# A hybrid decoder trunk on one core: triangles for the solve leave in two parts and are fetched by ScalarE

## The chip, the core and the metric

The kernel runs on one core of a Trainium2 chip. The core has five engines that run side by side, each with a queue of its own that is worked off in order: TensorE (PE, with its weight loads as PEld), VectorE (DVE), ScalarE (ACT), GpSimd (POOL) and SyncE (SP). SP does nothing but issue DMAs here; ACT and POOL can issue DMAs too, from their own queues. A DMA waits in the queue of the engine that issues it, and what stands behind it in that queue waits as well. The metric is device time in microseconds; less is better.

## The reference

One inference step of a two-layer trunk. Layer 0 is sliding-window attention, layer 1 is RWKV-7 time mixing, each between an RMS norm and a residual add, with a last RMS norm behind both. A prompt of 2048 tokens with 16 learned meta tokens ahead of it, and eight decoding sequences of four tokens, both go through it. The change lies in the recurrence of layer 1, which is by token and head

```
S_t = S_{t-1} diag(w_t) + (S_{t-1} a_t) b_t^T + v_t k_t^T ;   y_t = S_t r_t
```

with 16 heads of 64 by 64 states. Behind it y is normalised by head (mean and variance over 64 values, "group norm"), scaled, shifted, a bonus times v is added, the sum is multiplied by a SiLU gate and projected out, and the final norm follows.

## The kernel before

The kernel has four stages: attention, the mixing of neighbouring tokens, the dense projections of the recurrence's inputs, and the recurrence with all that stands behind it. The change is in the last one and in the helpers that it shares with the third.

**Units and chunks.** The recurrence is worked in units of 128 tokens: unit 0 holds the meta tokens, units 1 to 16 the prompt (`us`), and the decoding sequences follow at the end. A unit has four chunks of 32 tokens (unit 0 has one). Within a chunk the recurrence is a triangular system: `scores` (L948) multiplies keys and queries of two chunks at a time (`c2` is 0 or 1), copies the strictly triangular part of the result for each head to the tile `LAs` on ACT (L969) and, after a `yield`, writes the masked rest back into `L` on DVE.

**The inversion.** `inverse` (L976) inverts the 64 triangles of a unit (16 heads by 4 chunks, 32 by 32 each) at once. To have one triangle per partition it writes `LAs` to DRAM (`la_d`, L982 to L984, two DMAs from ACT), reads it back as `LA` into two halves of the partitions (L1007; on SP from unit 3 on), reads the norms `ln` and an identity `X` (L1008, L1010), multiplies `LA` by `ln` (L1009), and does the substitution row by row with two small operations each (`XT`, `X`, L1025 and L1026), on POOL for the units in question. At the end it scales `X` and writes it to DRAM (`tt_d`, L1030). `load_TT` (L1335) reads it back as `TT`, which the solve of the unit needs. `inverse` is a generator: it yields before the read back and at rows 8, 16, 22 and 26, and what stands between two yields is one portion.

**The serial part.** `chain` (L1425) is one chunk: products with the state into `C`, a copy `R0s` on ACT, then `solve` (L1397), small products with `TT` and four copies into `Z` on ACT, then the new state from `LS` and `Z`. `LS` are the keys, transposed on PE by `keys` (L1377) and copied by ACT, eight copies for two chunks; they are ahead of the solves that need them.

**What lies around it.** `steady` (L1770) writes out the order of units 2 to 14. For unit i and its chunk ch it interleaves: the chain of i; the scores of unit i+2, `s` in the code (c2 = 0 at the end of the second chunk, c2 = 1 in the third); the inversion of unit i+1, started while unit i-1 was worked, in its last portions, and of unit i+2 in its first ones; the group norm of unit i-1 (`group_norm`, L1587, in portions that end with MARK); the gate of unit i-1 (`gate`, chunks 2 and 3) and the projection out of unit i-2 (`project_out`, chunks 0 and 1), which are most of PE's work. Two tiles `vt` (L1595) hold v for the group norm; the next unit's loads wait until the last sums (L1643) have read them.

**What sets the order.** The kernel is written in one order, and a planner with a model of the engines' times then places the instructions of each engine. From unit 2 on `in_order` (L1757) ties DVE, ACT and POOL to the order as written, ACT's DMA issues among them; PE and SP are left to the planner. `released()` (L1408) holds what is written under it back, in the plan, until the last instructions of the chain have been issued. So the order on SP is the planner's and is fixed when the kernel is built; on the chip an instruction of SP that waits holds all behind it.

Of the kernel before, what the change touches and what calls it, by code (L numbers as in the profile page):

```python
# [30 lines left out]
def tile_hybrid_step(ctx: ExitStack, tc: tile.TileContext, a, o, c):  # L31
# [916 lines left out]
    def scores(u, c2):  # L948
# [22 lines left out]
        for e in range(2):  # L971
            for cc in range(w):
                r0 = 64 * cc
                tt(v_, L[OS[e], e, cc], pss[e][r0:r0 + 64], mk[r0:r0 + 64, None, :].broadcast_to([64, KC, 64]), ALU.mult)

    def inverse(u, room=None, ln=None):  # L976

        nch = u.nch
        nl = nch * 16
        la_d = dramr.tile([2, nl // 2, 32, 32], F32, name="la_d", tag=f"la_d{nch}")  # L980
        u.tt_d = tt_d = dramr.tile([32, 4, 4 * nch * 32], F32, name="tt_d", tag=f"tt_d{nch}")
        for e in range(2):  # L982
            dma(la_d[e].rearrange("l j i -> j l i"),
                u.LAs[32 * e:32 * e + 32].rearrange("p h c g i -> p (h c g) i"), s_)  # L984
        yield
        eng = v_ if u.idx == 1 else g_
        if u.kind == "m":
            room = wl.tile([P, 2, 32 * 32], F32, name="roomm", tag="L", bufs=nbuf["L"])
        if room is not None:
            LA = room[:, 0].rearrange("p (j i) -> p j i", i=32)  # L990
            XX = room[:, 1].rearrange("p (a k i) -> p a k i", a=2, i=32)
        else:

            LA = wk.tile([P, 32, 32], F32, name="LA", tag="LA", bufs=2)
            XX = None
        if XX is None:
            X = wk.tile([P, 16, 32], F32, name="X", tag="X", bufs=2)
            XT = wk.tile([P, 16, 32], F32, name="XT", tag="XT")
        else:
            X, XT = XX[:, 0], XX[:, 1]  # L1000
        if ln is None:
            ln = wp.tile([P, 32], F32, name="ln", tag=("mu", "rst0")[u.idx % 2])
        if nch < 4:
            g_.memset(LA, 0.0)
            g_.memset(ln, 1.0)
        for hh in range(2):
            dma(LA[hh * 64:hh * 64 + nl], la_d.rearrange("e l j i -> (e l) j i"), s_ if u.idx < PRE else None)  # L1007
            dma(ln[hh * 64:hh * 64 + nl], ln_d[u.idx].rearrange("q c g i -> (q c g) i"))  # L1008
        tt(eng, LA, LA, ln.unsqueeze(2).broadcast_to([P, 32, 32]), ALU.mult)  # L1009
        dma(X, c["laneid"])  # L1010

        low = 16 if u.kind == "m" else 0

        part = {2: 16}.get(u.idx, 0)
        cut = [(v_, 0, part), (g_, part, 16)] if 0 < part < 16 else [(v_, 0, 16)] if part else [(eng, 0, 16)]
        for j in range(low, 31):
            if j in (8, 16, 22, 26):
                yield
            w = 3 - j % 4 if u.kind == "s" else 31 - j
            for eng, k0, k1 in cut if w else ():  # L1020
                ks = slice(max(low // 2, k0), min(j // 2 + 1, k1))
                shape = [P, ks.stop - ks.start, w]
                if shape[1] <= 0:
                    continue
                tt(eng, XT[:, ks, :w], LA[:, j:j + 1, j + 1:j + 1 + w].broadcast_to(shape), X[:, ks, j:j + 1].broadcast_to(shape), ALU.mult)  # L1025
                tt(eng, X[:, ks, j + 1:j + 1 + w], X[:, ks, j + 1:j + 1 + w], XT[:, ks, :w], ALU.add)  # L1026
        for eng, k0, k1 in reversed(cut):
            u.inverted = tt(eng, X[:, k0:k1], X[:, k0:k1], ln[:, None, :].broadcast_to([P, k1 - k0, 32]), ALU.mult)
        for hh in range(2):
            dma(tt_d[hh:32:2].rearrange("k q (l i) -> (q l) k i", i=32), X[hh * 64:hh * 64 + nl])  # L1030
# [11 lines left out]
    with ExitStack() as ph:  # L1042
# [144 lines left out]
        for x, b in enumerate(order):  # L1187
# [39 lines left out]
            if follow is None:  # L1227

                if delay:
                    todo.append((b, prv))  # L1230
                    rest_v = rest_values()
                    fill(rest_v, V0)
                wrx.close()
                es = wrx.enter_context(tc.tile_pool(name="es", bufs=1, side="right", reuse_waits="tile"))
                wl = wrx.enter_context(tc.tile_pool(name="wl", bufs=1, side="right", reuse_waits="tile"))
                for u in us[:PRE]:
                    for _ in load_vectors(u):
                        pass
                if nblk > 2:
                    banks = lambda u: [pd.tile([P, KC, 64], F32, name="pz", tag="pd") for _ in range(2)]  # L1240
                    las = wk.tile([P, 2048], F32, name="las", tag="dx", bufs=1)
                    room1 = wk.tile([P, 2, 1024], F32, name="room1", tag="xn", bufs=1)
                    for i, x0, room in ((1, 0, room1), (0, 1024, None)):
                        u = us[i]
                        u.LAs = las[:64, x0:x0 + 256 * u.nch].rearrange("p (h c g i) -> p h c g i", h=2, g=4, i=32)
                        for c2 in range(u.np):
                            all_of(scores(u, c2))
                        for _ in inverse(u, room, las[:, x0 + 1024 - 32:x0 + 1024] if i == 0 else las[:, 1536:1568]):
                            pass
            if follow is not None:  # L1250
# [18 lines left out]
    with ExitStack() as ph:  # L1269
# [71 lines left out]
        def elementwise(u):  # L1341
            load = idle() if u.L else load_vectors(u)
            next(load, None)
            small_loads(u)
            if u.tt_d is None:
                new_LAs(u)
                for c2 in range(u.np):
                    all_of(scores(u, c2))
                    next(load, None)
                    yield 0.8  # L1350
                for _ in inverse(u):
                    pass
            load_TT(u)
            yield 0.8
# [22 lines left out]
        def keys(u, c2):  # L1377

            w = min(2, u.nch - 2 * c2)
            if u.kind == "s":  # L1380
                u.LS[c2] = [u.room[:, 1]]
            else:
                u.LS[c2] = [LSs[(LScount[0] + cc) % 4] for cc in range(w)]
                LScount[0] += 2
            pss = [pz.tile([P, 4, 2, 64], F32, name="kt", tag="pz") for _ in range(2)]
            for half, ps in enumerate(pss):
                for j in range(4):
                    t_.transpose(out=ps[:w * 64, j].rearrange("p e d -> p (e d)"),
                                 in_=u.BK[half][:, j, 2 * c2:2 * c2 + w, :].rearrange("p c x -> p (c x)"), identity=ident)
            yield  # L1390
            for half, ps in enumerate(pss):
                hs = slice(half * 4, half * 4 + 4)
                for cc in range(w):
                    for e in range(2):
                        act(u.LS[c2][cc][OS[e], e, hs, :], ps[cc * 64:cc * 64 + 64, :, e, :])

        def solve(u, ch, Z, R0s, out):  # L1397

# [371 lines left out]
        def steady(i, u, pe):  # L1770
# [9 lines left out]
            for ch in range(4):  # L1780
# [4 lines left out]

                left = rests[::-1]
                del rests[:]
                if ch == 3:
                    run(norm)
                with released():  # L1790
                    if ch == 2:
                        next(inv.get(i + 1, idle()), None)
# [19 lines left out]
                        run(gen)  # L1812
                if ch == 2:
                    with released():
                        inv[s.idx] = inverse(s)
                        next(inv[s.idx])
                        all_of(sc)
                run(pe[ch], 1.2)
                next(rec)
                with released():  # L1820
                    if ch == 0:
                        kt = keys(u, 1) if i > 2 else idle()
                        next(kt, None)
                        first = L0s.pop(s.idx, None)
                        load_BK(s)
                        s.L.append(first or load_L(s, 0))
                        all_of(kt)
                    if ch == 3:
                        all_of(kt)
                        next(inv[s.idx])  # L1830
                    else:
                        next(inv.get(i + 1, idle()), None)
                if ch < 2:
                    run(norm, to=MARK)
                elif ch == 3:
                    run(norms_[u.idx], to=MARK)
                run(pe[ch], 1.9)
                next(rec, None)
                with released():
# [3 lines left out]
                    if ch == 2 and i + 1 in inv:  # L1843
                        load_TT(us[i + 1])
                if ch == 2:
                    norms_[u.idx] = group_norm(u)
                    run(norms_[u.idx], to=MARK)
                    if ch == 3 and i + 3 < len(us):
                        L0s[i + 3] = load_L(us[i + 3], 0, s_)
# [3 lines left out]
                if ch == 1:  # L1853
                    with released():
                        new_LAs(s)
                        all_of(scores(s, 0))
                rests.append(pe[ch])
                for part in PLAN.get((i, ch), ()):
                    with released():
# [214 lines left out]
```

## Time and profile before

| | |
|---|---|
| Time, median of 3 runs | 2522.64 us (2521.0 to 2528.43) |
| The profiled execution's own time | 2526.93 us |
| Its span in the profile | 2525.2 us |
| Busy share of PE, DVE, ACT, POOL | 89%, 66%, 46%, 41% |
| Mean granted clock of PE | 0.958 |
| Instructions | 60868 |

In the profile's rows a tile name stands with an arrow to what it was made from, so `LA<-la_d` is the fetch of the triangles and `LA<-LA,ln` the first operation of an inversion; `xN` counts instructions. A row of the timeline gives start and duration in microseconds, engine, line, operation and shape, and in square brackets how long the engine had stood idle ahead of it and what it was put down to. ACTq and SPq are the queues of ACT and SP that issue DMAs; their durations are those of the issue, not of the transfer. A row of windows gives, for one stretch, its length, the busy time and number of instructions of PE, PEld, DVE, ACT and POOL, then PE's granted clock, the DMA engines' mean busy share and GB/s. A row of waits gives total, number of times and the longest one. Many lines are helpers: L38 is any matmul, L41 any activation, L44 any tensor_tensor, L47 any scalar_tensor_tensor, L50 any DMA. A wait for several things is put down to the one that came last by the profile, which can be the wrong one. The profile is of one execution and its times don't add up to those of another.

### The profile page before, as it was taken

To read this page: it belongs to the slowest core of one execution; us is meant where nothing else is said; L and a number is where in the kernel's file an instruction comes from. 1 tells how busy PE (TensorE), PEld (TensorE's weight loads), DVE (VectorE), ACT (ScalarE), POOL (GpSimd) and SP (SyncE) were. 2 spreads that over 40 slices of the span, in tenths; PEclk is the share of its full clock that TensorE was granted. 3 is DMA by queue.
4 is the path that set the end of the run, shared out by engine and by line. 5 is a ranking of instruction groups with operands and counts; after the bars stand their busy time and mean duration, and the time that the engine had idled before them with its cause. 6 is when DMAs were issued, how large, how long until landed. Compare 5 with 4: busy or idle time off the path is not lost. (4 is left out here: it accounts for less than half of the span.)

```text
span 2525.2 us, 60868 instructions
## 1 busy us (share of the span) xinstructions
PE 2238.5 (89%) x24932; PEld 1539.7 (61%) x24932; DVE 1666.3 (66%) x3181; ACT 1169.9 (46%) x2799; POOL 1035.9 (41%) x1572
## 2 busy tenths in 40 slices
PE   6989989899989897899999999666898888888897
PEld 5877768677855445577776668444555555555553
DVE  6586674577656987866556656555666666666674
ACT  6675465566432433554343444333444444445431
POOL 4242132333111334543333334314776766767613
PEclk9999999999999998899999999777999999999998
DMA  9433122333247564432222222575555655655323
GB/s 207 126 105 108 64 80 80 112 99 100 98 130 224 198 223 164 138 85 89 96 85 93 98 81 92 162 199 156 130 122 143 147 122 143 144 130 155 94 61 75
DMA packets 346234, 312.98 MB, mean 124 GB/s; under 512 B 205546, under 2 KB 282218, under 8 KB 344131
## 3 DMA queue, kind: packets, MB, share of 16 engines
q1 hardware_dynamic: 302515, 286.15, 38.4%
q10 hardware_dynamic: 41824, 19.15, 3.6%
q0 software_dynamic: 1616, 3.79, 0.7%
q8 instruction: 196, 3.21, 0.5%
q14 instruction: 83, 0.68, 0.1%
HBM read 191.15 MB, written 119.84 MB: 123 GB/s over the span
## 5 line engine op out<-in xcount | busy, mean ns | idle before, releaser
L38 PEld LDWEIGHTS <-yp 128*128 128x128 f16 x1488 | 141.4, 99 | 166.5 <-issue 13.4
L47 DVE SCALAR_TENSOR_TENSOR xm<-dx,mu,xn 128x256 f32<-128x256 f32 (+2 forms) x432 | 199.6, 521 | 48.4 <-POOL dx L44 47.1
L44 POOL TENSOR_TENSOR X<-X,XT 128x126 f32<-128x126 f32 (+24 forms) x458 | 186.1, 406 | 35.7
L44 POOL TENSOR_TENSOR XT<-LA,X 128x126 f32<-128x126 f32 (+24 forms) x458 | 179.7, 392 | 40.4 <-issue 6.7
L38 PE MATMUL pd<-xp,wq 128*128 128x256 f16 (+2 forms) x1728 | 186.7, 267 | 10.4 <-DVE qp L47 8.0
L38 PE MATMUL pd<-wg,xg 128*128 128x512 f16 (+1 forms) x816 | 193.5, 385 | 0.0
L38 PE MATMUL po<-wo,yp 128*128 128x512 f16 x768 | 191.3, 392 | 0.0
L38 PE MATMUL pd<-wvv,xpr 128*128 128x512 f16 (+1 forms) x816 | 189.1, 389 | 0.0
L38 PE MATMUL pd<-xpr,w 128*128 128x256 f16 (+2 forms) x1728 | 186.3, 267 | 0.0
L38 PE MATMUL pd<-xp,wg 128*128 128x256 f16 (+2 forms) x1728 | 181.9, 266 | 1.3 <-DVE xp L44 0.9
L38 PEld LDWEIGHTS <-wq 128*128 128x128 f16 x1728 | 159.5, 99 | 32.9 <-DVE qp L47 9.5
L38 PE MATMUL pd<-xpr,wkk 128*128 128x256 f16 (+2 forms) x1728 | 179.5, 264 | 0.0
L44 POOL TENSOR_TENSOR ssb<-ssb,bias 128x512 f32<-128x512 f32 x64 | 86.3, 1354 | 225.9 <-DVE ssb L462 185.4
L38 PEld LDWEIGHTS <-w 128*128 128x128 f16 x1728 | 157.8, 99 | 27.1 <-issue 9.7
L38 PEld LDWEIGHTS <-wg 128*128 128x128 f16 x1728 | 158.8, 99 | 21.7 <-issue 4.5
L38 PEld LDWEIGHTS <-wkk 128*128 128x128 f16 x1728 | 158.2, 98 | 15.6 <-issue 0.4
L38 PE MATMUL pd<-w,yp 128*128 128x512 f16 x720 | 162.3, 383 | 4.4 <-DMA yp<-y 4.4
L44 POOL TENSOR_TENSOR ps<-wst,ps 128x1024 f16<-128x1024 f32 x32 | 69.4, 2169 | 219.6 <-ACT wst L41 195.7
L44 DVE TENSOR_TENSOR Z<-C,pe 64x256 f32<-64x256 f32 x256 | 108.0, 422 | 61.0 <-PE C L38 42.9
L38 PEld LDWEIGHTS <-xpr 128*128 128x128 f16 (+1 forms) x816 | 79.2, 100 | 103.0 <-issue 18.3
L44 DVE TENSOR_TENSOR xpr<-xm,xpr 128x512 f16<-128x512 f32 (+2 forms) x144 | 98.9, 708 | 56.9 <-ACT xpr L41 56.6
L41 ACT ACTIVATE ssb<-ssb,ng 128x128 f32<-128x128 f32 (+1 forms) x272 | 104.2, 384 | 58.5 <-DVE es L44 54.8
(357 smaller groups left out, 4686.0 us busy)
## 6 DMA issues: line engine op xcount, KB each, us to landing
wst<-in_rwkv_w_in SPq DMA_DIRECT2D x32, 512.0 KB
wsp<-ps SPq DMA_DIRECT2D x32, 512.0 KB
BK<-bk SPq DMA_DIRECT2D x32, 512.0 KB
x<-in_x_prompt SPq DMA_DIRECT2D x29, 512.0 KB
xn<-xn SPq DMA_DIRECT2D x14, 1028.0 KB
ar<-aro SPq DMA_DIRECT2D x28, 512.0 KB
bk<-bko SPq DMA_DIRECT2D x28, 512.0 KB
L<-ar SPq DMA_DIRECT2D x38, 256.0 KB
```

The lines of the kernel that those rows point to most:

```text
L38: return t_.matmul(out=out, lhsT=lhsT, rhs=rhs, start=start, stop=stop, **kw).ins
L41: return s_.activation(out=out, in_=in_, func=func, **kw).ins
L44: return e.tensor_tensor(out=out, in0=in0, in1=in1, op=op).ins
L47: v_.scalar_tensor_tensor(out=out, in0=in0, scalar=scalar, in1=in1, op0=op0, op1=op1)
```

## The change

Four things in one edit.

- A new helper, `lanes_out`, writes the triangles to DRAM in two parts, one for each pair of chunks, each part as four DMAs (two row groups by two halves of the heads) where there were two for the whole unit. In `steady` the first part leaves at the end of the second chunk, ahead of the masked write-back, and the second part in the third chunk. For prompt units above 3 (`inner`: index over PRE, which is 3) they are issued by SP, for the others by ACT as before.
- `inverse` loads `ln` and the identity first and then yields; the read of `LA` comes in a second portion, which for `inner` units is issued by ACT, in the third chunk of unit i behind its solve, and then yields again. The multiplication of `LA` and the first rows stay in the fourth chunk.
- The last portion of the group norm, the sums with `vt`, moves from the start of the fourth chunk to the end of the third, ahead of the loads of the next `vt`.
- `keys` yields after each half of its copies. In a unit's first chunk the second half now comes after the portion of the group norm that has the squares and the variance.

```diff
+    def lanes_out(u, parts):
+
+        nl = u.nch * 16
+        if 0 in parts:
+            u.la_d = dramr.tile([2, nl // 2, 32, 32], F32, name="la_d", tag=f"la_d{u.nch}")
+        for c2 in parts:
+            w = min(2, u.nch - 2 * c2)
+            for e in range(2):
+                for h in range(2):
+                    l0 = (h * u.nch + 2 * c2) * 4
+
+                    dma(u.la_d[e, l0:l0 + 4 * w].rearrange("l j i -> j l i"),
+                        u.LAs[32 * e:32 * e + 32, h, 2 * c2:2 * c2 + w].rearrange("p c g i -> p (c g) i"), None if inner(u) else s_)
+
+    def inner(u):
+        return PRE < u.idx and u.kind == "p"
+
     def inverse(u, room=None, ln=None):
...
-        la_d = dramr.tile([2, nl // 2, 32, 32], F32, name="la_d", tag=f"la_d{nch}")
+        la_d = u.la_d
...
-        for e in range(2):
-            dma(la_d[e].rearrange("l j i -> j l i"),
-                u.LAs[32 * e:32 * e + 32].rearrange("p h c g i -> p (h c g) i"), s_)
-        yield
...
         for hh in range(2):
-            dma(LA[hh * 64:hh * 64 + nl], la_d.rearrange("e l j i -> (e l) j i"), s_ if u.idx < PRE else None)
             dma(ln[hh * 64:hh * 64 + nl], ln_d[u.idx].rearrange("q c g i -> (q c g) i"))
+        dma(X, c["laneid"])
+        yield
+        for hh in range(2):
+            dma(LA[hh * 64:hh * 64 + nl], la_d.rearrange("e l j i -> (e l) j i"), s_ if inner(u) or u.idx < PRE else None)
+        if inner(u):
+            yield
         tt(eng, LA, LA, ln.unsqueeze(2).broadcast_to([P, 32, 32]), ALU.mult)
-        dma(X, c["laneid"])
...
                     for e in range(2):
                         act(u.LS[c2][cc][OS[e], e, hs, :], ps[cc * 64:cc * 64 + 64, :, e, :])
+                yield
...
                 del rests[:]
-                if ch == 3:
-                    run(norm)
...
                 if ch == 2:
                     with released():
+                        lanes_out(s, (1,))
                         inv[s.idx] = inverse(s)
                         next(inv[s.idx])
                         all_of(sc)
...
-                        all_of(kt)
+                        next(kt, None)
                     if ch == 3:
                         all_of(kt)
                         next(inv[s.idx])
                     else:
                         next(inv.get(i + 1, idle()), None)
+                    if ch == 2 and s.idx > PRE:
+                        next(inv[s.idx])
                 if ch < 2:
                     run(norm, to=MARK)
+                if ch == 0:
+                    with released():
+                        all_of(kt)
                 elif ch == 3:
                     run(norms_[u.idx], to=MARK)
...
                 if ch == 2:
+                    run(norm)
                     norms_[u.idx] = group_norm(u)
...
                 if ch == 1:
                     with released():
                         new_LAs(s)
-                        all_of(scores(s, 0))
+                        sc = scores(s, 0)
+                        next(sc)
+                        lanes_out(s, (0,))
+                        all_of(sc)
```

Where `inverse` is called for units 0 to 3 outside `steady` (L1248 and L1351), a call of `lanes_out` for the parts now stands ahead of it, in `elementwise` after each pair of scores.

More of the change, by code (lines that the diff above doesn't have):

```diff
@@ L1247, in tile_hybrid_step @@
                             all_of(scores(u, c2))
+                        lanes_out(u, range(u.np))
                         for _ in inverse(u, room, las[:, x0 + 1024 - 32:x0 + 1024] if i == 0 else las[:, 1536:1568]):
@@ L1348, in elementwise @@
                     all_of(scores(u, c2))
+                    lanes_out(u, (c2,))
                     next(load, None)
```

## The prediction

> **What bounds the kernel now.** I read the page first, for which stage is long and what its chain is made of.
>
> ```profile
> span 2525.2 us, 60868 instructions
> PE 2238.5 (89%) x24932; PEld 1539.7 (61%) x24932; DVE 1666.3 (66%) x3181; ACT 1169.9 (46%) x2799; POOL 1035.9 (41%) x1572
> POOL 4242132333111334543333334314776766767613
> POOL 12%; PE 7%; DMA 5%; issue 3%; SPq 2%; DVE 1%; ACT 1%; ACTq 0%; POOLq 0%; DVEq 0%
> ```
>
> PE is busiest over the whole span, but the chain that ended last is mostly POOL. POOL is near 70% busy in slices 28 to 37 alone: that is the recurrence. Next come the groups on tile LA from 1750 us on, the busy times of the eleven units that lie between its first and its twelfth multiplication, and the waits of PE in the same stage.
>
> ```profile
> L44 POOL TENSOR_TENSOR LA<-LA,ln x13: 1910/1912/1914, 1761.7 to 2320.1; 128x1024 f32<-128x1024 f32 x13
> ...
> 1761.70:2274.20 512.50, 450.62 (x8374) 272.61 (x8369) 343.01 (x552) 233.66 (x592) 359.82 (x759) 0.97 0.56 135
> ```
>
> ```profile
> PE C L38 <- DMA TT<-tt_d: 21.8, 13, 3.3
> PE yps L1676 <- DVE gt L44: 13.8, 12, 1.2
> PE C L38 <- issue: 12.6, 9, 1.9
> PE C L38 <- ACT Z L41: 10.1, 14, 1.3
> ```
>
> Thirteen inversions start from 1761.7 to 2320.1, so a unit takes 558.4/12 = **46.53 us**. In the eleven whole units PE is busy 450.62/11 = 41.0 us each, POOL 32.7. The four waits, from 1750 to 2280 us (530/46.53 = 11.4 units), are 1.9, 1.2, 1.1 and 0.9 us of PE per unit: with the 41.0 they make 46.1, nearly the whole unit. Now one unit in order of time on POOL, SP, ACT, PE and DVE.
>
> ```profile
> 1985.47 1.28 POOL L44 TENSOR_TENSOR X<-X,ln 128x512 f32<-128x512 f32 x1
> 1994.84 1.91 POOL L44 TENSOR_TENSOR LA<-LA,ln 128x1024 f32<-128x1024 f32 x1 [8.08 <-DMA Z<-v]
> ...
> 2011.61 0.20 POOL L1623 TENSOR_SCALAR var<-var 128x16 f32<-128x16 f32 x1 [0.40 <-DVE var L1620]
> ...
> 2031.81 1.27 POOL L44 TENSOR_TENSOR X<-X,ln 128x512 f32<-128x512 f32 x1
> ```
>
> ```profile
> 1986.78 1.36 SPq L50 DMA_DIRECT2D tt_d<-X  x2
> 1988.19 1.33 SPq L50 DMA_DIRECT2D ln<-ln  x2
> 1989.63 1.17 SPq L50 DMA_DIRECT2D LA<-la_d  x2
> 1990.90 1.10 SPq L50 DMA_DIRECT2D TT<-tt_d  x2
> ...
> 1992.57 1.06 SPq L50 DMA_DIRECT2D vt<-v  x2
> ```
>
> ```profile
> 1980.21 0.94 ACTq L50 DMA_DIRECT2D la_d<-LAs  x2
> 1981.19 1.56 ACT L41 ACTIVATE Z<-C 32x256 f32<-32x256 f32 x4 [1.01 <-issue]
> 1985.58 0.60 ACT L41 ACTIVATE gt<-pd 128x512 f32<-128x512 f32 x1 [2.82 <-PE pd L38]
> ...
> 2006.61 2.32 ACT L41 ACTIVATE LS<-kt 64x256 f32<-64x256 f32 x6 [0.21 <-PE kt L1388]
> ...
> 2009.62 0.58 ACT L41 ACTIVATE Y<-ytm 128x512 f32<-128x512 f32 x1
> ```
>
> POOL ends one inversion at 1986.75 and then stands 8.08 us until the next unit's triangle is in LA. The wait is put down to Z<-v, but LA's own DMA explains it: the triangle left for DRAM at 1980.21 from the ACT queue, and its fetch was issued on SP only at 1989.63, because SP's queue stood behind tt_d<-X, which needs the end of the inversion before. The single microseconds below show that the triangle had been moved by then: the DMA engines are busy from 1981 to 1983 and empty after it.
>
> ```profile
> 1982.00:1983.00 1.00, 0.87 (x20) 0.73 (x22) 0.49 (x2) 0.74 (x2) 0.84 (x3) 1.00 0.56 91
> 1983.00:1984.00 1.00, 1.00 (x19) 0.66 (x17) 0.97 (x3) 0.00 (x0) 0.77 (x4) 1.00 0.00 0
> ...
> 1992.00:1993.00 1.00, 1.00 (x14) 0.46 (x14) 0.97 (x3) 0.96 (x3) 0.00 (x0) 1.00 1.11 279
> ```
>
> A second loop has almost the same length; these are its rows on PE and DVE.
>
> ```profile
> 1988.88 0.66 PE L1676 MATMUL yps<-ident,gt 128*128 128x128 f32 x4 [1.15 <-DVE gt L44]
> ...
> 2002.08 1.06 PE L38 MATMUL C<-R0s,TT 32*32 32x64 f32 x28 [3.33 <-DMA TT<-tt_d]
> ```
>
> ```profile
> 1986.21 0.69 DVE L47 SCALAR_TENSOR_TENSOR gt<-gt,pd 128x512 f32<-128x512 f32 x1 [1.74 <-ACT gt L41]
> 1986.81 1.28 DVE L44 TENSOR_TENSOR ytm<-ytm,vt 128x512 f32<-128x512 f32 x2
> 1988.13 0.69 DVE L44 TENSOR_TENSOR gt<-gt,ytm 128x512 f32<-128x512 f32 x1
> ...
> 2006.38 1.41 DVE L44 TENSOR_TENSOR ytm<-Y,mean 64x512 f32<-64x512 f32 x2
> 2010.23 1.29 DVE L1620 TENSOR_REDUCE var<-Y 128x8 f32<-128x512 f32 x2 [2.44 <-ACT Y L41]
> ```
>
> From the inversion's end at 1986.75 its result goes out as tt_d and back as TT, and PE can solve at 2002.08: 15.3 us. From there to the end of the variance's reduction on DVE at 2011.52 it is 9.4. POOL, whose next operation in its order is that variance, then needs until 2033.08, 21.5. Together 46.2: POOL waited only 0.40 us at var, so this **TT loop** ties with the LA wait. Removing the LA wait alone would only move POOL's stand to var.
>
> **The change, part by part.** *The fetch.* For units 4 to 16 LA<-la_d leaves SP, and is issued on ACT between the third chunk's Z copies (end 1982.75) and its gate (1985.58). The second part's four writes, now on SP, wait for copies that end at 1980.2. Their price: a pair of the same bytes took 0.94 us to issue, so 0.9 to 1.9 for four, I take 1.3 (about 0.3 each); and by the rows above some 2 us to land: 1983.5. The fetch is 1.17 to issue and was in use 5.2 us after its issue (1989.63 to 1994.84): 1988.7, which is 2.0 after the inversion's end, not 8.1. The first part's writes leave a chunk earlier and are covered by the scores and solve of that chunk. ACT is held for the landing from 1982.75 to about 1983.5 and needs 1.2 for the issue, inside its 2.82 wait for PE; queued behind it are gt, R0s and everything of the fourth chunk, so this cover is thin. SP's eight small writes cost it 2.6 us of issue per unit while nothing else is due.
>
> *Around TT.* With LA's two reads (512 KB) off SP's queue, TT no longer lies behind them: at 279 GB/s (row 1992) that is up to 1.9 us. ln and laneid also go before tt_d now; the 1.33 and 1.17 us of issue between tt_d and TT may have been covered by tt_d's own landing, so they are worth 0 to 2.5. Against it, vt is free earlier, and its 512 KB could go out ahead of tt_d: a loss of up to 1.9. Ends -1.9 and +4.4, I take a gain of 1.0: that of half of LA's bytes.
>
> *Squares.* Eight key copies take 3.1 us (2.32 for six); the squares now follow the first four, so the first starts at about 2006.61 + 1.55 = 2008.16, when ytm is ready (2007.79), not at 2009.62: 1.5 us earlier, with the var behind it. The four later copies then end 1.2 us later, which their reader, the state update, can bear or not: 0 to 1.2, I take 0, since in this unit that update was waiting for po's matmuls around it.
>
> *The last sums.* The two additions of vt (1.28) go from between the gate's two DVE steps to the idle 1.74 ahead of them. The product is ready 1.3 earlier and PE's wait of 1.15 at yps goes: 1.2 per unit on PE, 0 if another wait takes its place.
>
> *Start.* Units 0 to 3 keep ACT for everything, and their triangles now go in four DMAs per part. For units 0 and 1 that is 8 more on the path to the first solve.
>
> ```profile
> 1604.74 1.01 ACTq L50 DMA_DIRECT2D la_d<-las  x2
> 1606.20 4.39 ACTq L50 DMA_DIRECT2D la_d<-las  x2
> 1610.93 1.14 ACTq L50 DMA_DIRECT2D room<-la_d  x2
> ```
>
> At 0.3 to 0.5 each this is 2.4 to 4.0; part of it may vanish in the 4.39, where ACT's queue waited anyway. Ends 0 and 4, I take a loss of 2.0.
>
> *The sum.* Three limits for the new unit. PE: 41.0 busy, none of which the change removes; with the waits for TT and yps gone but the other two and small ones kept (about 2.2): 43.2. TT loop: 14.3 + 7.9 + 21.5 = 43.7. LA, over two units: from TT's arrival to the second part's writes 26.7 (2002.08 to the next unit's 2028.8, below), 8.5 for out and back as above, 38.2 of POOL (1994.84 to 2033.08), 14.3 for TT's trip: 87.7, or 43.9 for one.
>
> ```profile
> 2028.79 0.94 ACTq L50 DMA_DIRECT2D la_d<-LAs  x2
> ```
>
> I take the longest, 43.9: a gain of 2.6 in each of 12 units, 31.6, less 2.0 at the start, **29.6 us**. The profiled execution took 2526.93 (span 2525.2, 1.7 around it) and would take 2497.3; the median of the runs shown lies 4.3 lower, so 2493.
>
> By the Trainium skill (DMA: Bandwidth & Descriptors, "Issuing engines are not separate DMA queues") DMAs from SP and ACT run on the same 16 engines, and issuing from two of them saves just the time of issue. That speaks against expecting more than 1.17 us a unit here; but the rows show a wait in SP's order, not a shortage of engines (none busy in 1983). Its result is the fourth rival.
>
> **The rivals.** *Better.* TT's trip shrinks by more than 2 and PE's remaining waits halve as units close up: PE is at 41.0 + 1.1 = 42.1, a gain of 4.4 x 12 - 2 = 51: 2472. For it: PE's other waits are called issue and Z, which are matters of order. Against: PE would be 97% busy, as it is nowhere in this stage.
>
> *Hidden anyway.* POOL reaches var early and stands there, because TT's trip stays at 15.3 and the squares wait for something else. For it: the loop's 46.2 against 46.5 today. Then only a few tenths, say 0.5 a unit, are left: 2522.6 - 6 + 2 = 2519.
>
> *Slower.* The change doesn't do what it says: the planner puts the second part's writes behind tt_d in SP's order. Then SP holds them until 1986.75, they are out at 1989.4 and landed at 1991.4, LA is there at 1996.6 instead of 1994.8, and ACT, which stands at the fetch, lets the gate through at 1992.6 and not 1985.6. POOL's part alone is 1.8 x 12 + 2: 2546, more if PE starves. It loses from the point where the writes land later than 1989.6, today's issue of the fetch. For it: SP stands in order for long.
>
> ```profile
> SPq L50 <- POOL X L44: 94.0, 11, 10.3
> ...
> SPq L50 <- DMA la_d<-LAs: 9.4, 1, 9.4
> ```
>
> Against: in the code these writes come before the third chunk's solve, and POOL's last steps are released only after it, so tt_d should be planned later.
>
> *Issue time only.* If the transfers stay as slow as now and only SP's 1.17 of issue is saved per unit: 14 - 2 = 12, 2511.
>
> **How the numbers follow.** Forecast 0.58, better 0.10, hidden 0.15, slower 0.11, issue only 0.06. The forecast's own range is a unit of 43.2 to 45.0: 2485 to 2506. About 0.3% (7.6 us) is what a measurement of this kernel can tell from no change. Faster by more: the forecast, better, issue only, and half of hidden, 0.81. Within: the other half, 0.08. Slower: 0.11. The range 2474 to 2522 takes in half of better and all of hidden and leaves out slower: about 0.16 outside.
>
> **What would show it.** LA multiplications 43 to 45 us apart; POOL's idle time before LA 2 us or less, with some of it now before var; LA<-la_d on the ACT queue before tt_d<-X on SP; PE's wait at yps near zero, at TT smaller; the squares among the LS copies. The forecast is wrong if the unit stays above 45.5 although POOL no longer waits at LA (then the TT loop did not shrink), if ACT's wait before gt grows past 3 us with the fetch in front of it, or if the gain is lost between 1600 and 1700 us.

## The result and the profile after

The changed kernel takes 2508.43 us in the median of four runs, the kernel before 2523.29 in the same comparison: a ratio of 0.993, 95% interval 0.9916 to 0.9944, so about 15 us less. The forecast was 2493, some 30 less. The profiled execution took 2505.96 us, 21.0 less than that of before; it lies 2.5 under its median, that of before 3.6 over its own, so the two profiles differ by more than the medians do.

The page of the changed kernel:

```profile
span 2504.2 us, 61036 instructions
PE 2247.1 (90%) x24932; PEld 1543.8 (62%) x24932; DVE 1676.0 (67%) x3181; ACT 1169.6 (47%) x2799; POOL 1035.7 (41%) x1572
POOL 4242132233111333533333333314677777777613
```

PE's and POOL's work are the same; the slices of the recurrence are fuller. The inversions of units 4 to 16, and POOL's waits from 1768 to 2246 us, of the changed kernel (the columns of a wait are total, times, longest):

```profile
L44 POOL TENSOR_TENSOR LA<-LA,ln x13: 1910/1912/2104, 1765.9 to 2300.3; 128x1024 f32<-128x1024 f32 x13
```

```profile
POOL LA L44 <- DMA LA<-la_d: 36.4, 8, 5.9
POOL var L1643 <- DVE var L1640: 14.2, 9, 2.2
POOL LA L44 <- DMA TT<-tt_d: 6.7, 1, 6.7
POOL LA L44 <- DMA ln<-ln: 5.0, 1, 5.0
```

and those of the kernel before in the same stretch:

```profile
POOL LA L44 <- DMA Z<-v: 68.7, 8, 9.1
POOL LA L44 <- DMA LA<-la_d: 16.6, 2, 8.8
POOL var L1623 <- DVE var L1620: 1.5, 2, 1.1
```

A unit takes 534.4/12 = 44.53 us where it took 46.53. POOL's wait at LA fell from 85.3/10 = 8.5 to 48.1/10 = 4.8 us a unit, and a new stand at var came in, 1.4 where there was 0.2. One unit of the changed kernel on POOL, SP, ACT, PE and DVE:

```profile
2158.46 1.26 POOL L44 TENSOR_TENSOR X<-X,ln 128x512 f32<-128x512 f32 x1
2163.98 1.91 POOL L44 TENSOR_TENSOR LA<-LA,ln 128x1024 f32<-128x1024 f32 x1 [4.26 <-DMA LA<-la_d]
...
2182.23 0.20 POOL L1643 TENSOR_SCALAR var<-var 128x16 f32<-128x16 f32 x1 [1.92 <-DVE var L1640]
...
2202.75 1.27 POOL L44 TENSOR_TENSOR X<-X,ln 128x512 f32<-128x512 f32 x1
2208.47 1.91 POOL L44 TENSOR_TENSOR LA<-LA,ln 128x1024 f32<-128x1024 f32 x1 [4.44 <-DMA LA<-la_d]
```

```profile
2159.75 1.57 SPq L50 DMA_DIRECT2D tt_d<-X  x2
2161.38 2.65 SPq L50 DMA_DIRECT2D ln<-ln  x2
2166.15 1.09 SPq L50 DMA_DIRECT2D TT<-tt_d  x2
...
2194.12 2.95 SPq L50 DMA_DIRECT2D la_d<-LAs  x4
...
2199.00 3.00 SPq L50 DMA_DIRECT2D la_d<-LAs  x4
```

```profile
2178.78 1.55 ACT L41 ACTIVATE LS<-kt 64x256 f32<-64x256 f32 x4
2180.23 0.58 ACT L41 ACTIVATE Y<-ytm 128x512 f32<-128x512 f32 x1
...
2199.78 1.56 ACT L41 ACTIVATE Z<-C 32x256 f32<-32x256 f32 x4
2203.52 1.11 ACTq L50 DMA_DIRECT2D LA<-la_d  x2
2204.68 0.60 ACT L41 ACTIVATE gt<-pd 128x512 f32<-128x512 f32 x1 [3.34 <-PE pd L38]
```

```profile
2174.05 0.64 PE L38 MATMUL C<-R0s,TT 32*32 32x64 f32 x28 [2.07 <-DMA TT<-tt_d]
```

```profile
2180.85 1.29 DVE L1640 TENSOR_REDUCE var<-Y 128x8 f32<-128x512 f32 x2 [0.61 <-ACT Y L41]
```

The fetch of the triangles stands on ACT at 2203.52, ahead of the inversion's end at 2204.02 and not behind it, as meant. The TT loop can be read off: from the inversion's end (2159.72) to PE's solve 14.3 us, to the end of the variance on DVE (2182.14) 8.1, to the next inversion's end 21.9, together 44.3, which is the unit. POOL stood 1.92 us at var in it, so in this unit the TT loop ended last, and the wait at LA did not.

Three lengths serve for all runs below. They count from the last product of the projections, `k<-aa,k` on POOL, since the stages ahead of it are the same code in all kernels and yet end up to 15 us apart (1583.5 to 1598.5).

```profile
1589.56 0.73 POOL L44 TENSOR_TENSOR k<-aa,k 128x256 f32<-128x256 f32 x1 [2.71 <-ACT aa L41]
```

```profile
1587.02 0.73 POOL L44 TENSOR_TENSOR k<-aa,k 128x256 f32<-128x256 f32 x1 [2.71 <-ACT aa L41]
```

(Kernel before, then changed kernel.) "Start" runs from there to LA of unit 4, "unit" is a twelfth of the time from there to LA of unit 16, "end" runs from there to the end of the span. All ratios are against the kernel before on the same chip.

| kernel | start | unit | end | ratio | 95% interval |
|---|---|---|---|---|---|
| before | 172.2 | 46.53 | 205.1 | 1 | |
| changed | 178.9 | 44.53 | 203.9 | 0.9930 | 0.9916 to 0.9944 |
| 1 fetch only | 179.4 | 45.43 | 207.1 | 0.9991 | 0.9976 to 1.0006 |
| 2 squares and sums only | 174.0 | 47.18 | 206.5 | 1.0024 | 1.0009 to 1.0038 |
| 3 one part | 175.2 | 43.77 | 205.4 | 0.9895 | 0.9875 to 0.9915 |
| 5 TT in four DMAs | 167.7 | 41.94 | 203.7 | 0.9778 | 0.9762 to 0.9793 |
| 6 start as before | 173.3 | 44.27 | 207.5 | 0.9908 | 0.9893 to 0.9923 |
| 7 fetch on SP | 178.1 | 45.22 | 202.0 | 0.9977 | 0.9967 to 0.9988 |
| 8 = 3, 5 and 6 | 158.4 | 41.80 | 204.7 | 0.9746 | 0.9730 to 0.9761 |
| 9 no squares | 179.4 | 45.71 | 204.9 | 0.9982 | 0.9969 to 0.9996 |
| 10 no sums | 177.3 | 44.44 | 205.3 | 0.9922 | 0.9901 to 0.9943 |
| 11 before, TT in four DMAs | 155.8 | 46.27 | 204.7 | 0.9919 | 0.9904 to 0.9934 |

Of the 21 us between the two profiles, 24.0 were gained in the units, 6.7 lost at the start, 1.2 gained at the end and 2.5 lie ahead of the recurrence.

Start, unit and end are read from one execution of each kernel, and the profiled ones lie between 6.0 us under the median of their kernel (run 7) and 10.0 over it (run 2). Start, twelve units and end, added up and compared with the first row, agree with the medians within 8 us. By this a unit is known to about half a microsecond (an estimate), and smaller differences in that column say little; the ratios come from all executions.

### The profile page after: what moved, and what is told of

The parts are those of the page before. It is cut to its first block, busy times and chain, and to the rows that moved or that the text cites. A ratio compares the mean times of both kernels' runs of the same rounds, so it can differ in the third digit from the quotient of the medians.

```text
span 2504.2 us, 61036 instructions
## 1 busy us (share of the span) xinstructions
PE 2247.1 (90%) x24932; PEld 1543.8 (62%) x24932; DVE 1676.0 (67%) x3181; ACT 1169.6 (47%) x2799; POOL 1035.7 (41%) x1572
## 4 chain that ended last, share of the span: by engine, by line
PE 34%; DVE 19%; DMA 14%; POOL 14%; ACT 10%; issue 6%; SPq 3%; ACTq 1%; POOLq 0%; DVEq 0%
PE pd L38 23%; DVE xm L47 4%; POOL X L44 4%; POOL XT L44 3%; SPq L50 3%; PE po L38 3%; DMA tt_d<-X 2%; DVE xpr L44 2%; ACT ssb L41 2%; DMA wst<-in_rwkv_w_in 2%; DMA TT<-tt_d 1%; PE sc L38 1%; PE C L38 1%; POOL var L44 1%; DMA vt<-v 1%
## 5 line engine op out<-in xcount | busy, mean ns | idle before, releaser
L38 PE MATMUL pd<-wg,xg 128*128 128x512 f16 (+1 forms) x816 | 200.2, 394 | 0.0
L38 PEld LDWEIGHTS <-wkk 128*128 128x128 f16 x1728 | 158.2, 98 | 15.6 <-issue 0.4
L38 PEld LDWEIGHTS <-xg 128*128 128x128 f16 (+1 forms) x816 | 77.1, 101 | 90.9 <-issue 13.9
```

The source lines that it names most:

```text
L38: return t_.matmul(out=out, lhsT=lhsT, rhs=rhs, start=start, stop=stop, **kw).ins
```

## The experiments

**1. The fetch without the rest, and 2. the rest without the fetch.** In the first, from the changed kernel:

```diff
-                        next(kt, None)
+                        all_of(kt)
...
-                if ch == 0:
-                    with released():
-                        all_of(kt)
...
-                    run(norm)
                     norms_[u.idx] = group_norm(u)
```

with `run(norm)` back at the fourth chunk; the second is the kernel before with just these three edits made.

> The changed kernel with the squares and the last sums of the norm put back to their old places; the two-part writes and ScalarE's fetch stay. Theory (two loops tied: the LA wait and the TT loop): POOL no longer waits long at LA but stands 3 to 4 us at var, the TT loop is 44.2 + 1.5 for the squares = 45.7, the unit 45.5 to 46, so 5 to 10 us less than the 2523 of before: 2513 to 2518. Rival (the LA wait was the cause by itself): the whole gain stays, 2506 to 2510.

> The kernel before with only the squares between the key copies and the norm's last sums at the third chunk's end; the triangles leave and come back as before. Theory (tied loops): POOL still waits 8 us at LA each unit, the unit stays at 46.3 to 46.5, time 2519 to 2524, no change to be told. Rival (PE's wait for gt, 1.2 us a unit, is gained by itself): 14 us less, 2509.

The fetch alone gives nothing that can be told in time (0.9991), where 5 to 10 us were expected; its unit is 1.1 us shorter, about as expected, and the start, 7.2 us longer, takes most of that back. Two rows of its POOL show the stand at var beside the shorter one at LA:

```profile
2092.98 2.63 POOL L44 TENSOR_TENSOR LA<-LA,ln 128x1024 f32<-128x1024 f32 x1 [4.08 <-DMA Z<-v]
2112.33 0.20 POOL L1643 TENSOR_SCALAR var<-var 128x16 f32<-128x16 f32 x1 [2.32 <-DVE var L1640]
```

The rest alone gains nothing either; it is slower by 0.24%, where no change was expected. (Its unit of 47.18 is from the slowest of twelve executions.) POOL still waits 8 us at LA:

```profile
2192.42 1.91 POOL L44 TENSOR_TENSOR LA<-LA,ln 128x1024 f32<-128x1024 f32 x1 [8.10 <-DMA LA<-la_d]
```

So neither edit alone brings the gain, and both are needed, as two tied loops would have it. Why the second is slower and not equal I don't know: PE's waits for ACT's Z are 31.1 us from 1768 to 2246 where they were 8.3, and POOL is busy 373.5/11 = 34.0 us a unit where it was 32.7.

**9. Without the squares, 10. without the sums.** The same edits, one at a time, taken out of the changed kernel.

> The changed kernel with the squares put back behind all eight key copies. Theory (the TT loop sets the changed kernel's unit, and the squares lie in it): the unit grows by 1 to 1.5 us, 45.5 to 46, time 10 to 16 us over the changed kernel, 2518 to 2524. Rival (the last sums carried the part that the fetch alone did not give): within 3 us of the changed kernel, 2505 to 2512.

> The changed kernel with the norm's last sums put back to the start of the fourth chunk. Theory: they lie on PE's way to yps and not in the TT loop, so PE waits 1 us more at yps, in a stand that the TT loop has anyway: the unit stays within 0.5 of 44.5, time 2506 to 2514. Rival (the sums carried it): 10 to 14 us over the changed kernel, 2519 to 2522.

The squares carry what the fetch alone lacked: without them the unit is 45.71, 1.2 us longer, POOL stands 32.7/11 = 3.0 us at var, and the time, 2519.78 us, is what was expected. The sums carry nothing that can be measured: 44.44. Without them PE's waits at yps are 16.7 us in all (1770 to 2250) where the changed kernel has 4.7 (1768 to 2246), and the time is the same within the two intervals.

**3. One part.** In `lanes_out`:

```diff
+        if inner(u):
+            for e in range(2) if 1 in parts else ():
+                dma(u.la_d[e].rearrange("l j i -> j l i"),
+                    u.LAs[32 * e:32 * e + 32].rearrange("p h c g i -> p (h c g) i"))
+            return
```

> The changed kernel, but for the units from 4 on the triangles leave in one part, two DMAs on SP after the last copies, where there were eight in two parts. Theory (the fetch's place matters, and the TT loop sets the unit): the two writes take 1 to 1.5 us of issue and not 3.0, LA is there at the same time or 1 us earlier, the unit stays at 44 to 44.7, time 2504 to 2512. Rival (the first part's early leaving is what makes the fetch early): twice the bytes land 2 us later, the unit grows by 1 us, 2520.

It is faster than the changed kernel, by more than either view allowed for: 0.9895, a unit of 43.77. The writes on SP, the gate on ACT behind the fetch, and the next operation of POOL:

```profile
2193.62 1.59 SPq L50 DMA_DIRECT2D la_d<-LAs  x2
```

```profile
2198.79 0.60 ACT L41 ACTIVATE gt<-pd 128x512 f32<-128x512 f32 x1 [2.82 <-PE pd L38]
```

```profile
2201.76 2.51 POOL L44 TENSOR_TENSOR LA<-LA,ln 128x1024 f32<-128x1024 f32 x1 [3.05 <-DMA tt_d<-X]
```

From the first to the last, two writes of 128 KB take 1.59 us here, and the four of 32 KB took 3.00. These rows hold gaps and slow single issues; the issues one by one, first in the changed kernel, then in run 3 on SP, then in the kernel before on ACT (shortest, median and longest in ns):

```profile
L50 SPq DMA_DIRECT2D la_d<-LAs x104: 303/442/2125, 1748.1 to 2292.6; - x104
L50 SPq DMA_DIRECT2D la_d<-LAs x26: 318/332/1598, 1750.2 to 2282.3; - x26
L50 ACTq DMA_DIRECT2D la_d<-LAs x24: 322/323/577, 1746.2 to 2260.6; - x24
```

A quarter of the bytes is not issued faster: 0.44 us in the median against 0.33. On SP single writes also take up to 2.1 and 1.6 us; in the row of 3.00 one of the four took 1.61. Why, no run shows. The change doubled the number of writes behind the last copies, and the part that leaves early saves nothing that counts.

How that reaches the unit can be read on ACT. In the kernel before, in run 3 and in run 7 ACT waits 2.8 us for PE ahead of the first gt of every unit from 1800 to 2250. In the changed kernel, where the fetch on ACT first waits for the small writes, it is 2.8 to 3.8 us, and over 3 in eight of eleven units. So ACT is held there, 0.4 us a unit in the mean, only where the small writes and the fetch on ACT come together. That this is all of the 0.76 us between the two units is not shown.

**6. The start as before.** The same edit with `not inner(u)` and ScalarE as issuer.

> The changed kernel, but the triangles of units 0 to 3 leave whole, by two DMAs from ScalarE as before. Theory (the start lost 7 us to the many small writes): LA of unit 4 is multiplied 4 to 7 us earlier counted from the last projection, the unit stays at 44.5, time 4 to 7 us less than the changed kernel, about 2502. Rival (the start is late for another reason, the new order of its loads): within 2 us of the changed kernel.

The start is 5.6 us shorter, 173.3, and the time, 2500.63 us, is what was expected (the ratio is 0.9908; its interval overlaps that of the changed kernel). The many small writes were most of the loss at the start; the new order of the loads was not.

**7. The fetch on SP.**

```diff
-s_ if inner(u) or u.idx < PRE else None)
+s_ if u.idx < PRE else None)
```

> The changed kernel with LA fetched by SP; all else stays, the two-part writes too. Theory (what counts is that the fetch does not stand behind tt_d in SP's order; the planner puts it behind tt_d here): POOL waits 8 us at LA again, the unit is 46.4 to 47, time 2524 to 2534. Rival (only the issue time of 1.2 us a unit is saved by ScalarE): 1.2 times 12 = 14 us over the changed kernel, 2522; rival (the two parts and the new order bring the gain): no change from 2508.

The planner did put the fetch behind tt_d, but the wait came back only in part:

```profile
2163.81 1.35 SPq L50 DMA_DIRECT2D tt_d<-X  x2
2165.33 2.62 SPq L50 DMA_DIRECT2D LA<-la_d  x2
...
2169.16 1.09 SPq L50 DMA_DIRECT2D TT<-tt_d  x2
```

POOL waits 6.2 to 7.4 us at LA, not 8, and never stands at var; the unit is 45.22. So 1.3 of the 2.0 us a unit are there without ScalarE's fetch. The rows show one reason: ln no longer lies between tt_d and the fetch, which is issued 1.5 us behind tt_d's first issue and not 2.85. No run changes the place of ln alone. The move to ScalarE gives the remaining 0.7 us a unit by the profiles; by the medians it is 10 us, 0.8 a unit. The fourth rival had put the saved issue at 1.17. These are too near each other for this run to say whether ScalarE saves more than its issue: the wait at LA falls by 1.9 us, from 6.7 in the mean to 4.8, and 1.4 of it come back as the stand at var. My expectation for this run missed by a microsecond a unit, and in time (2518.04) the rival of the issue, 2522, was nearer.

**5. TT in four DMAs, and 11. the same in the kernel before.**

```diff
             for gh in range(2):
-                dma(u.TT[64 * gh:64 * gh + 64].rearrange("p c g i -> p (c g i)"), u.tt_d[:, gh:4:2].rearrange("k q x -> q k x"))
+                for j in range(2):
+                    r0 = 64 * gh + 32 * j
+                    dma(u.TT[r0:r0 + 32].rearrange("p c g i -> p (c g i)"), u.tt_d[:, gh + 2 * j])
```

> The changed kernel, with TT read back by four DMAs of 32 rows each, where two DMAs had an outer dimension of 2 and kept about two DMA engines busy. Theory (the TT loop of 44.2 sets the unit): TT lands 3 to 4 us earlier, the TT loop is 41, and the unit is next set by LA's loop over two units or by PE, at 42.5 to 43.5: 12 to 24 us less than the changed kernel, 2484 to 2496. Rival (PE is the floor at 44.5 with its small waits): 2504 to 2512, PE's waits come back elsewhere.

> The kernel before with TT read by four DMAs of 32 rows, no other change. Theory (two tied loops: the LA wait keeps the unit by itself): POOL waits 8 us at LA, the unit stays at 46.0 to 46.5; the start, where TT's trip is waited for one unit at a time, gains about 11 us as it did in the changed kernel with this edit: 2508 to 2515. Rival (TT's trip was the one bound of the unit before too): the unit falls to 42 to 43, 2460 to 2480.

Number 4 was the edit of run 5 with a slip in its text and gave no time.

This is the test of the TT loop, and the largest gain here. In the kernel before, while PE waited for TT, the 16 DMA engines were busy to 0.14, about two of them (in a row of windows the last two columns are DMA share and GB/s):

```profile
2000.00:2001.00 1.00, 0.00 (x0) 0.00 (x0) 0.00 (x0) 0.00 (x0) 0.84 (x3) 1.00 0.14 51
```

The Trainium skill (DMA: Bandwidth & Descriptors, "Why a DMA increments its semaphore by 16 and not by 1") says that a DMA is split over the largest number of engines, up to 16, that divides the slowest dimension of both its sides. TT's was 2; the share of 0.14 agrees. In the changed kernel other transfers fill the engines meanwhile (a share of 0.83 from 2172 to 2173, while PE waits), so there only the edit can tell. With 32 rows first, SP and PE of run 5 read:

```profile
2090.99 1.35 SPq L50 DMA_DIRECT2D tt_d<-X  x2
...
2094.41 1.72 SPq L50 DMA_DIRECT2D TT<-tt_d  x4
```

```profile
2097.73 0.64 PE L38 MATMUL C<-R0s,TT 32*32 32x64 f32 x28 [0.31 <-DMA TT<-tt_d]
```

From tt_d's issue to the solve it is 6.7 us here, not 14.3. This is the only unit between 1758 and 2220 in which PE still stood for TT, 0.3 us; the changed kernel's PE stood 10.9 in all. The unit falls to 41.94 and the time to 0.9778, 2466.25 us, below the 2484 to 2496 that I had expected: the unit is half a microsecond under my range, and the start gains 11.2 that I had left out. PE is then busy 437.86 of 461.71 us, 95%:

```profile
1758.34:2220.05 461.71, 437.86 (x8355) 264.54 (x8354) 349.74 (x547) 231.20 (x589) 369.39 (x760) 0.99 0.60 149
```

In the kernel before, the same edit leaves the unit at 46.27, because POOL goes on waiting at LA:

```profile
2156.39 1.92 POOL L44 TENSOR_TENSOR LA<-LA,ln 128x1024 f32<-128x1024 f32 x1 [8.38 <-DMA LA<-la_d]
```

POOL's own round, the wait at LA and the inversion behind it, was 46.3 us long in the prediction's rows of the kernel before (1986.75 to 2033.08), and TT has no part in it. Run 11 gains 16.4 us at the start, more than the 11 I expected there. So a shorter TT trip is worth 2.6 us a unit with the LA wait lowered, and 0.3 without.

**8. Three edits together.** Runs 3, 5 and 6 in one kernel, the triangles of all units in one part.

> The changed kernel with three edits together: triangles of every unit in one part by two DMAs (on SP from unit 4 on, on ScalarE below), and TT read by four DMAs. Theory: the gains add up where they lie in different places, start 4 to 7, one part 11, TT on top until PE or LA's loop binds at 42.5 to 43: 2480 to 2490. Rival (PE is the floor at 43.8): 2492 to 2497.

2458.59 us, 0.9746, the fastest here and below the 2480 to 2490 expected, since the start falls to 158.4, 20.5 less than in the changed kernel. The gain of one part is gone in the units (41.80 against 41.94). PE is busy 434.96 of 457.89 us there, 95%, which fits PE as the limit; no run tests that.

## Why the prediction was right, and where its sizes were off

**What bounds.** Right in the main. The two tied loops are what runs 1, 2, 9 and 11 show: with edits for one loop alone the unit is 1.1 us shorter at best (0.7 longer in run 2, 0.3 shorter in run 11), and with edits to both it is 2.0 or 4.6 shorter. But of the three limits the forecast took the wrong one for the longest, LA's loop over two units. In the unit shown that loop comes to 25.0 (2174.05 to 2199.00), 9.5 (to 2208.47), 38.1 of POOL (2163.98 to 2204.02 less the stand of 1.92) and 14.3: 86.9, or 43.4 for one, about as forecast. The TT loop was longer, 44.3 and not 43.7, and POOL stands at var in nine of the ten units from 1800 to 2246, which says the same.

**The sum.** A unit of 43.9 was forecast, and 44.53 measured, inside the 43.2 to 45.0 given for it; 29.6 us in all, and 21.0 between the profiles or 15 between the medians, half of it. So 2508 lies just above the forecast's own 2485 to 2506 and inside the wide range. Four terms were mis-sized.

- *The four writes*, "0.9 to 1.9 for four, I take 1.3": 3.00 in the unit shown. The pair that gave the price was not "of the same bytes", as I wrote: it moved 256 KB and the four move 128. And it was priced from ACT's queue, where an issue took 0.32 us in the median; on SP it was 0.44, with single ones of up to 2.1. With that the fetch is issued at 2203.52, and the wait at LA is 4.8 in the mean, not 2.0. One of the signs of being wrong that I had named came with it, ACT's wait before gt past 3 us (3.34 in the unit shown); it cost tenths of a microsecond a unit and not the gain. Run 3, with 1.59, has a unit of 43.77, the forecast's size.
- *Around TT*, "a gain of 1.0" on the trip of 15.3: the unit shown has 14.3, but that is the luck of the unit. Over the seven units in which PE stood for TT the trip is 14.1 to 15.4 from tt_d's issue, 14.7 in the mean, and over the eleven such units of the kernel before it is 14.0 to 15.6, 14.9 in the mean. One reason stands in the rows: the planner left ln behind tt_d (2161.38, 2.65 us), where I had counted on it going ahead. And SP now waits for tt_d to land before it can issue TT, 19.6 us in ten times from 1768 to 2246, where it had waited 0.2.
- *The start*, "ends 0 and 4, I take a loss of 2.0": 6.7, above the upper end. The price of one write held, 0.31 us in the median on ACT for units 0 and 1. Yet by the first multiplication of unit 1 (`room`, 26.5 us from the last projection before, 30.6 after) 4.1 us are lost, by that of unit 3 2.2, and by that of unit 4 6.7. So most of it comes in behind unit 3's start, and units 2 and 3, with small writes of their own on ACT, had been left out of the count. Run 6 gets 5.6 back; which of the writes cost it is open.
- *PE*, "the waits for TT and yps gone": those for TT are not, 10.9 us from 1768 to 2246, and those for ACT's Z rose from 8.3 to 12.1 in the same stretch. It was not the longest of the three limits, so it cost nothing here.

**The other terms.** In the unit shown tt_d to TT's issue took 6.4 us where it took 4.1, and TT itself 7.9 where it took 11.2. The squares were put at 1.5, measured 1.3 in the trace and 1.2 by run 9. The sums of the norm were given 1.2 us of PE; its wait at yps fell by 0.7 a unit (from 11.5 to 4.7 us in all from 1768 to 2246). In the sum they had no part, since PE was not the limit; run 10 bears that out.

**The rivals.** *Slower* did not come: the writes stand ahead of tt_d on SP in all units. *Hidden anyway* is what the fetch does by itself (run 1). *Better* is what happens once TT's trip is short (run 5); against it I had held that PE would be 97% busy "as it is nowhere in this stage", which was no reason: PE gets to 95% in run 5, and its busy time a unit falls from 41.0 to 39.8 with the granted clock at 0.99 and not 0.97. *Issue time only* forecast 2511, nearer the median than my 2493. For ScalarE's own part, 0.7 to 0.8 us a unit by run 7, it is not ruled out. It does not explain the whole: run 7 keeps 1.3 us a unit without ScalarE, and run 9, with ScalarE but without the squares, keeps 0.8 of the 2.0.

**What I did not see.** The trip of TT was in front of me, in a trace that has a DMA share near two engines at its end, and I bounded its gain by what the change does to it. It was the largest thing to be had in this stage.

## What to carry to other kernels

Where two loops have the same length, an edit to one of them can measure as nothing, as runs 1 and 2 did; compute both from the trace before a change is dropped, and try the edits together. When a transfer is late, look at the DMA share while it is awaited: here a share of 0.14 went with an outer dimension of 2, and the bandwidth was not the limit. More and smaller DMAs on a path cost their issue each (here 0.44 us at 32 KB and 0.33 at 128 KB), so a part that leaves early must save more than the added issues take. And a queue that also feeds compute, as ACT's does, is held by a DMA that has to wait.

## What the runs showed of the hardware that I had not expected

Reading 256 KB as two DMAs with an outer dimension of 2 took 9.7 to 11.2 us from its issue to its use in the kernel before, in the eleven units in which PE stood for it, and as four DMAs of 32 rows 3.3 in the one such unit of run 5 (2094.41 to 2097.73). The issue of a write of triangles took 0.44 us of SP's queue in the median at 32 KB and 0.33 at 128 KB, and on ACT's queue 0.32 at 128 KB; on SP single ones took up to 2.1. The same early stages end up to 15 us apart between executions, so profiles of two kernels have to be compared from a common event in each.
